# A fused encoder block in float32 on one core: which PSUM banks row tiles take, where x1's transposes stand, and the order of the last writes

## The chip, the cores and the metric

The kernel runs on one core of one Trainium2 chip. The metric is the device time of one execution in microseconds (us); the number that counts is the median over several executions. A profiled execution is one more execution, recorded instruction by instruction by the hardware profiler.

## The reference: what is computed

One layer of an encoder with two attention mixers side by side, for x of shape 1 x 512 x 2048 in float32:

```python
h = rmsnorm(x, g_mix)
qa, ka, va, qb, kb, vb = split(h @ w_in)          # 1024, 256, 256, 1024, 1024, 1024 columns
out_a = rmsnorm(mixer_a(qa, ka, va, g_q_a, g_k_a), g_out_a)   # 8 query heads, 2 kv heads, axial rotary
out_b = rmsnorm(mixer_b(qb, kb, vb), g_out_b)                 # 8 heads, three dilated windows, partial rotary
x = x + concat(out_a, out_b) @ w_out
h2 = rmsnorm(x, g_ffn)
gate, up = split(h2 @ w_gate_up)                  # D_FF = 5632
x = x + (silu(gate) * up) @ w_down
return rmsnorm(x, g_final)
```

The input's 512 rows are four row tiles of 128. A product in float32 precision is made of three passes: each operand is split into a high and a low part, and `mm3` (L229 to L231) issues high x high, high x low and low x high into one PSUM bank.

## The kernel before

**The work in its order.** The first chunk makes kA and vA from w_in. Three column blocks make qA, vB and half of qkB out of sums of blocks of the operands (seven products in place of eight). Two plain chunks of `in_chunk` make the rest of qkB: a chunk has 512 output columns, sixteen units (one slice of 128 rows of w_in each), and in each unit four row tiles, one `mm3` each into a bank of its own. Then come the products with w_out, four chunks c = 0 to 3 for mixer A's half (`out_chunk` "A", whose units hold one slice of eight) and four for B's. Gate and up, down, and the final norm follow, in column blocks again.

**Attention beside it.** The attention's tasks stand in a list called `side`. While plain chunks and out chunks run, `give` hands out credit (2.8 for a unit, half of it after the second row tile, the rest at the end), and takes tasks from the front of `side` as long as the credit covers their cost. A task of mixer A's heads is a slot (`head_slot`): a score product, the softmax of an earlier one, transposes of p (L659) into a bank called pt, which ScalarE (L220) and VectorE (L221) copy out as pTh and pTl, and the product of p with the values. `weighed` attaches a cost to a task; in `wait(n)` n empty tasks are put into the list, each worth a unit outside the attention, where one unit gives a credit of 1.

**Banks.** PSUM has eight banks of 128 x 512, all in one queue, `banks`. `bank()` takes the one at the left, which was given back longest ago; `release` appends at the right. It is a queue of the program as it is written out: a bank is given back at the place where the instruction that reads it last is issued, and a new product in it waits on the chip until that instruction has run. A chunk takes its four banks at its first unit; `in_chunk`'s post evicts by ScalarE (L491, evqkB), `out_chunk`'s by VectorE (L1195, which scales and adds to x1).

**x1 and its transposes.** Behind the last unit of an out chunk B, x1's 512 columns are done, and `h_side` (L1236) transposes them piece by piece on TensorE (L1241, four 128 x 128 transposes for a piece). ScalarE copies them into `pair` with a gain (L1244), VectorE sums blocks of two pieces (L380), and ScalarE and VectorE split these into high and low parts (L1252, L1254). These tasks go through `side` as well, behind `wait(2)` for c = 0 and 1 and `wait(1)` for c = 2 and 3.

**The start.** In the first sixteen units `prepare` makes the high parts of the weights on ScalarE (L963) and the low parts on VectorE (L966), and `row_squares` (L388) has ScalarE square the rows of x for the first norm.

**The end.** `finish` does the last product's row tile 1 by itself: ScalarE squares it (L1532), VectorE adds up (L1534), GpSimd takes the power -0.5 (L1535), which gives the row scale r, and then the four column groups of the last row tile are scaled and written: three by `write` (L1506 on VectorE or L1508 on ScalarE, DMA at L1509), one straight out of PSUM (L1538 and L1540, DMA at L1541).

Of the kernel before, what the change touches and what calls it, by code (L numbers as in the profile page):

```python
# [20 lines left out]
P = 128  # L21
# [56 lines left out]
def encoder_block(ctx, tc, x, w_in, g_q_a, g_k_a, w_out, w_gate_up, w_down, g_final, x_t, gains, c_ident, c_mask,  # L78
# [27 lines left out]

    def bank():
        return banks.popleft()

    def release(*tiles):  # L110
        banks.extend(tiles)
# [627 lines left out]
    def attention_tasks():  # L739
        def q_tasks(j):  # L740
            return norm_rope(lambda t: (qA[j][t], qA[j][t]), 4, "q")

        def both(cost, *lists):
            return [weighed(cost, lambda fs=fs: [f() for f in fs]) for fs in zip(*lists)]

        qA.update({j: {} for j in range(2)})
        qkB.update({j: {} for j in range(4)})
        push_heads()
        k_squares, k_turned, k_scaled = norm_rope(lambda t: (kA[t][:, :256], kA[t][:, 256:]), NKV, "k")
        q_squares, q_turned, q_scaled = q_tasks(0)  # L750
        vs = [lambda t=t: split_vA(t) for t in range(NT)]
        tables = light(0.8, table_tasks())
        todo = tables[:3] + both(1.4, [lambda t=t: scale_k(t) for t in range(NT)], k_squares)
        todo += both(0.6, vs) + tables[3:]
        todo += both(2.0, q_squares, k_turned, k_scaled) + both(2.6, q_turned, q_scaled)
        todo += light(0.6, [lambda kv=kv: transpose_k_a(kv) for kv in range(NKV)]) + [heads[0].tq, heads[0].tk]
        todo += light(0.1, [lambda: reload("qA1", qA[1])])
        extra = {}

        def at(slot, tasks):  # L760
            extra.setdefault(slot, []).extend(tasks)
        at(20, light(0.1, [lambda: nc.sync.dma_start(mask, c_mask)]))
        q_squares, q_turned, q_scaled = q_tasks(1)
        for t in range(NT):
            at(t // 2, both(0.8, q_squares[t:t + 1]))
            at(2 + 2 * t, both(0.9, q_turned[t:t + 1]))
            at(3 + 2 * t, both(0.9, q_scaled[t:t + 1]))
        def turn_at(turned, slots):
            for t, s in enumerate(slots):
                at(s, light(0.05, [lambda t=t: turned.part(t)]))  # L770
                at(s + 1, light(0.05, [lambda t=t: turned.turn(t)]))
        turn_at(turned_a[0], (0, 1, 2, 2))
        turn_at(turned_a[1], range(4, 12, 2))
        for j in range(4):
            s = NT * (NHA + 2 * j)
            if 2 * j < TURNED_ON_PE["B"]:
                at(s - 11, light(0.1, [lambda j=j: reload(f"qkB{j}", qkB[j])]))
                at(s - 7, light(0.9, [lambda j=j: rope_partial(qkB[j]["whole"])]))
                continue
            at(s - 16, light(0.1, [lambda j=j: reload(f"qkB{j}", qkB[j])]))  # L780
            for n in range(2):
                at(s - 13 + n, light(0.45, [lambda j=j, n=n: rope_partial(qkB[j]["whole"], 2 * n, 2)]))
            turn_at(turned_b[j], range(s - 10, s - 6))
        for h in range(NHB):
            s = NT * (NHA + h)
            at(s + 2, light(0.1, [lambda h=h: load_vB(h)]))
            at(s + 4, light(0.4, [lambda h=h: split_vB(h)]))
        for s in range(2 * NHA * NT + VALUE_LAG + 2):
            cost = 1.5 if s < NHA * NT else 1.2 if s < 2 * NHA * NT else 0.7
            todo += [weighed(cost, lambda s=s: head_slot(s))] + extra.get(s, [])  # L790
        return todo

# [52 lines left out]
    def in_chunk(pieces, post):  # L845
        box = {}

        def mm(u, k):
            if k == 0:
                box["ps"] = [bank() for _ in range(NT)]  # L850
            by_rows(u, k, KD, lambda i, w, t: mm3(box["ps"][t], x_of(i, t), w, i == 0, i == KD - 1),
                    lambda rows: post(box["ps"], rows))
        add_chunk(w_in, [k * P for k in range(KD)], pieces, mm, None, tag="wi")
# [295 lines left out]
    def out_chunk(kind, c):  # L1149
# [28 lines left out]
        def mm(u, n):  # L1178
            k = order[n]
            if n == 0:  # L1180
                box["ps"] = [bank() for _ in range(NT)]
                if kind == "A":
                    whole = slot("x1", F32, (P, NT, 512))
                    x1[c] = [whole[:, t] for t in range(NT)]
                    for t in range(NT):
                        nc.sync.dma_start(x1[c][t], x[0, t * P:(t + 1) * P, c * 512:(c + 1) * 512])
            by_rows(u, n, NHA, lambda i, w, t: mm3(box["ps"][t], cols(oS[kind, order[i]], t * P), w, i == 0,
                                                   i == NHA - 1), post, kind == "A")

        def post(rows):  # L1190
# [7 lines left out]
                if kind == "B" and c < NC - 1:  # L1198
                    square_x1(c, t)
            if kind == "B" and NT - 1 in rows:  # L1200
                wait(2 if c < 2 else 1)
                if c == NC - 1:
                    side.extend(lambda p=p: h_side(2 * c, p, True) for p in range(4))
                    side.append(lambda: [square_x1(c, t) for t in (0, 1)])
# [30 lines left out]
    def h_side(i, half, apart=False):  # L1235
        if half < 2:  # L1236
            k = 2 * i + half
            c, j = divmod(k, 4)
            ps = bank()
            for n, t in enumerate((2, 3, 0, 1) if half == 0 else range(NT)):  # L1240
                nc.tensor.transpose(ps[:, n * P:(n + 1) * P], x1[c][t][:, j * P:(j + 1) * P], ident)  # L1241
            if half == 0 and not hpart:
                hpart[0] = sp.tile([P, 4 * 512], F32, tag="pair", bufs=1, name=nm("pair"))
            nc.scalar.activation(hpart[0][:, half * 1024:half * 1024 + 512], ps, AF.Copy, scale=gf[:, k:k + 1])  # L1244
            release(ps)
# [272 lines left out]
    def finish(box):  # L1518
# [14 lines left out]
        r = fin["r", 1] = m[:, 1:2]  # L1533
        nc.vector.tensor_tensor(m[:, 3:], m[:, :1], pre[:, 1:], op=OP.add)  # L1534
        nc.gpsimd.tensor_tensor(r, m[:, 3:], mhalf[:, :1], op=OP.pow)  # L1535
        write(1, 0, True, nc.sync)
        write(1, 2, False, nc.scalar)
        nc.vector.tensor_tensor(m[:, 2:3], r, r2["r"][:, 1:2], op=OP.mult)  # L1538
        write(1, 1, True, nc.sync)
        nc.vector.scalar_tensor_tensor(x1[3, 1], ps[1], m[:, 2:3], gfin[3], op0=OP.mult, op1=OP.mult)  # L1540
        nc.scalar.dma_start(out[0, P:2 * P, 3 * 512:], x1[3, 1])  # L1541

    box.after("m3", 40, lambda: evs.extend(held[name][:, t] for name in ("s1", "s7") for t in range(2)))
    first = 0
# [77 lines left out]
    for n, u in enumerate(units):  # L1622
        share["now"], share["due"] = n, 1.0
        if n < KD:
            if n + 5 < KD:
                load_x(n + 5)
            if n + 1 < KD:
                x_prep(n + 1)
        if n <= ROWS_AT[-1]:
            row_squares(n)  # L1630
        prepare(n)
        for v in units[n + 1:n + 3]:
            if v.early is not None:
                v.early()
                v.early = None
        u.mm(u)
        if u.post is not None:
            u.post()
        for f in hooks.pop(n, ()):
            f()  # L1640
        give(1.0)
# [57 lines left out]
```

## Time and profile before

| what | value |
| --- | --- |
| median of 3 runs | 1947.94 us (1947.91 to 1948.31) |
| profiled execution, its own time | 1947.76 us |
| span of its records | 1946.0 us |
| TensorE (PE) busy | 1932.1 us, 99% |
| VectorE (DVE) busy | 1537.4 us, 79% |
| ScalarE (ACT) busy | 1152.7 us, 59% |

Rows of a timeline are: start, duration, engine, line of the kernel, operation, output <- input, form, and in brackets the idle time before it and what ended it. A row with xN holds N instructions that follow each other, and its duration spans them all. Matmuls overlap: a matmul's row is longer than its distance to the next, so idle time of TensorE is best read from start to start. A list of waits has engine, line, what was waited for, total us, times, longest us. A row of windows has the window, its length, then busy time and count of TensorE, its weight loads, VectorE, ScalarE and GpSimd, the granted clock of TensorE, the DMA share and the bytes per second.

### The profile page before, as it was taken

Reading aid. Unit: us, or ns where it says so; the run is one execution under the profiler, and the core shown is the slowest. Engines: PE = TensorE matmul, PEld = TensorE weight load, DVE = VectorE, ACT = ScalarE, POOL = GpSimd, SP = SyncE. Lnnn points to the kernel's source line nnn. Section 1 sums busy time; section 2 is a strip of 40 time slices with the busy share of each in tenths; the row PEclk is TensorE's granted clock in tenths of the full one; section 3 lists DMA queues with packets and bytes.
Section 4 is the critical chain, followed back from the end, with each engine's and each line's share of the span. In section 5 each row is a group of like instructions: output and inputs, shape, how many; then the busy total and the mean of one; then the engine's idle time right before and its main releaser. Section 6 shows DMA issues by size and latency. Waiting matters only on the chain.

```text
span 1946.0 us, 24535 instructions
## 1 busy us (share of the span) xinstructions
PE 1932.1 (99%) x8687; PEld 1593.4 (82%) x8687; DVE 1537.4 (79%) x2020; ACT 1152.7 (59%) x1673; POOL 140.6 (7%) x184
## 2 busy tenths in 40 slices
PE   9999999999999999999999999999999999999998
PEld 7888887888888888888888888888888888888886
DVE  7987768888785697778778778787788978787886
ACT  7755556675765565555555555555555666555555
POOL 1000011000000000000000000000000121111121
PEclk9999999999999999999999999999999999999999
DMA  9676694354442556858658768678587798868865
GB/s 347 235 263 225 216 290 118 92 184 146 124 147 98 174 196 204 284 144 286 241 164 284 225 195 285 196 231 296 145 283 269 215 243 266 230 162 243 239 146 168
DMA packets 268924, 413.50 MB, mean 212 GB/s; under 512 B 75584, under 2 KB 102720, under 8 KB 268672
## 3 DMA queue, kind: packets, MB, share of 16 engines
q1 hardware_dynamic: 237968, 325.31, 51.6%
q0 software_dynamic: 22480, 60.57, 12.4%
q10 hardware_dynamic: 8352, 26.05, 4.1%
q8 instruction: 68, 1.11, 0.2%
q14 instruction: 56, 0.46, 0.1%
HBM read 334.52 MB, written 62.65 MB: 204 GB/s over the span
## 4 chain that ended last, share of the span: by engine, by line
PE 94%; DVE 3%; ACT 2%; issue 1%; DMA 0%; ACTq 0%; DVEq 0%; POOLq 0%; POOL 0%; SPq 0%
PE b L229 31%; PE b L231 30%; PE b L230 30%; PE b L659 1%; ACT rj L448 0%; DVE x L1195 0%; PE b L1241 0%; DVE w L307 0%; DVE ra L461 0%; ACT w L302 0%; DVE tw L966 0%; DVE qA L464 0%; DVE qA L470 0%; DMA stage<-in_w_in_dram 0%; DVE fixed L635 0%
## 5 line engine op out<-in xcount | busy, mean ns | idle before, releaser
L907 ACT ACTIVATE wide<-raw 128x1024 fp32r<-128x1024 f32 x462 | 487.1, 1058 | 457.6 <-PE b L231 269.6
L910 DVE TENSOR_TENSOR wide<-raw,wide 128x1024 fp32r<-128x1024 f32 x462 | 562.8, 1223 | 202.8 <-ACT wide L907 191.5
L229 PE MATMUL b<-wide,arena 128*128 128x512 f32 x1848 | 719.8, 390 | 0.0
L231 PE MATMUL b<-wide,arena 128*128 128x512 f32 x1848 | 719.2, 389 | 0.0
L230 PE MATMUL b<-wide,arena 128*128 128x512 f32 x1848 | 719.1, 389 | 0.0
L231 PEld LDWEIGHTS b<-wide,arena 128*128 128x128 f32 x1848 | 346.9, 188 | 72.3
L230 PEld LDWEIGHTS b<-wide,arena 128*128 128x128 f32 x1848 | 346.9, 188 | 71.7
L229 PEld LDWEIGHTS b<-wide,arena 128*128 128x128 f32 x1848 | 346.9, 188 | 71.7
L1043 DVE TENSOR_TENSOR raw<-raw,raw 128x1024 f32<-128x1024 f32 x264 | 321.6, 1220 | 7.0 <-DMA raw<-in_w_gate_up_dram 7.0
L230 PE MATMUL b<-tw,arena 128*128 128x512 f32 x396 | 154.3, 390 | 0.6 <-DVE tw L966 0.6
L231 PE MATMUL b<-tw,arena 128*128 128x512 f32 x396 | 154.2, 389 | 0.0
L229 PE MATMUL b<-tw,arena 128*128 128x512 f32 x396 | 154.1, 389 | 0.0
L963 ACT ACTIVATE tw<-stage 128x512 fp32r<-128x512 f32 x140 | 85.5, 629 | 69.3 <-DVE stage L1043 45.9
L966 DVE TENSOR_TENSOR tw<-stage,tw 128x512 fp32r<-128x512 f32 x140 | 93.9, 688 | 22.1 <-ACT tw L963 15.9
L229 PE MATMUL b<-w,arena 128*128 128x512 f32 x240 | 95.2, 397 | 0.0
L231 PE MATMUL b<-w,arena 128*128 128x512 f32 x240 | 93.9, 391 | 0.0
L230 PE MATMUL b<-w,arena 128*128 128x512 f32 x240 | 93.5, 390 | 0.0
L230 PEld LDWEIGHTS b<-tw,arena 128*128 128x128 f32 x396 | 74.3, 188 | 16.7 <-DVE tw L966 1.4
L231 PEld LDWEIGHTS b<-tw,arena 128*128 128x128 f32 x396 | 74.3, 188 | 15.9 <-DVE arena L354 0.4
L229 PEld LDWEIGHTS b<-tw,arena 128*128 128x128 f32 x396 | 74.3, 188 | 15.5
L380 DVE TENSOR_TENSOR pair<-pair 128x256 f32<-128x256 f32 x120 | 46.4, 423 | 46.7 <-ACT pair L1244 23.2
L220 ACT ACTIVATE pTh<-b 128x512 fp32r<-128x512 f32 x64 | 38.3, 598 | 64.4 <-PE b L659 62.5
(243 smaller groups left out, 2118.1 us busy)
## 6 DMA issues: line engine op xcount, KB each, us to landing
raw<-in_w_gate_up_dram SPq DMA_DIRECT2D x308, 512.0 KB, 6.3
raw<-in_w_down_dram SPq DMA_DIRECT2D x88, 512.0 KB, 7.4
stage<-in_w_in_dram SPq DMA_DIRECT2D x111, 256.0 KB, 5.4
forms<-pair POOLq DMA_DIRECT2D x22, 896.0 KB, 6.3
fr<-forms ACTq DMA_DIRECT2D x35, 512.0 KB, 5.3
raw<-in_w_out_dram SPq DMA_DIRECT2D x32, 512.0 KB, 4.2
x1d<-s POOLq DMA_DIRECT2D x54, 256.0 KB, 6.5
stage<-in_w_in_dram SPq DMA_DIRECT2D x90, 128.0 KB, 3.6
```

Of the source, the lines that this page charges most:

```text
L220: nc.scalar.activation(hi, src, AF.Copy)
L229: nc.tensor.matmul(dst, ah, bh, start=start, stop=False, skip_group_check=chained)
L230: nc.tensor.matmul(dst, ah, bl, start=False, stop=False, skip_group_check=chained)
L231: nc.tensor.matmul(dst, al, bh, start=False, stop=stop, skip_group_check=chained)
L380: nc.vector.tensor_tensor(out, x, y, op=op)
L659: nc.tensor.transpose(ps[:, t * P:(t + 1) * P], self.p[t][:, kb * P:(kb + 1) * P], ident)
L907: nc.scalar.activation(self.hi, self.src, AF.Copy)
L910: nc.vector.tensor_tensor(self.lo, self.src, f32(self.hi), op=OP.subtract)
L963: nc.scalar.activation(self.pair[:, 0], self.src, AF.Copy)
L966: nc.vector.tensor_tensor(self.pair[:, 1], self.src, f32(self.pair[:, 0]), op=OP.subtract)
L1043: nc.vector.tensor_tensor(t[dst], t[src[0]], t[src[1]], op=OP.add if form == "m6" else OP.subtract)
```

## The change

The change has these parts:

- `chunk_banks` takes two banks from the left of the queue for row tiles 0 and 1, and the two that were given back last, from its right, for row tiles 2 and 3. `in_chunk` uses it, and `out_chunk` for mixer A from c = 1 on.
- In the attention's list the head slots 2, 3 and 4 cost 1.65 where they cost 1.5.
- The first head's `tq` (first query's transposes) and `tk` change places: a `tk` of 0.7, `tq`, and an empty task of 0.3, where there were two tasks of 1.0.
- `wait(2)` for c = 2, which had `wait(1)`.
- In `h_side` the four transposes of a piece run in the order of the row tiles; only where the results stand in the bank is turned.
- In the first units `row_squares` stands behind `prepare` from unit KD = 16 on, up to which it stands ahead of it.
- In `finish` the last row tile's writes have another order and other queues.

```diff
+    def chunk_banks():
+        first = [bank() for _ in range(2)]
+        late = [banks.pop() for _ in range(2)]
+        return first + late[::-1]
...
-        todo += light(0.6, [lambda kv=kv: transpose_k_a(kv) for kv in range(NKV)]) + [heads[0].tq, heads[0].tk]
+        todo += light(0.6, [lambda kv=kv: transpose_k_a(kv) for kv in range(NKV)])
+        todo += [weighed(0.7, lambda: heads[0].tk()), heads[0].tq, weighed(0.3, lambda: None)]
...
-            cost = 1.5 if s < NHA * NT else 1.2 if s < 2 * NHA * NT else 0.7
+            cost = 1.65 if 2 <= s < 5 else 1.5 if s < NHA * NT else 1.2 if s < 2 * NHA * NT else 0.7
...
-                box["ps"] = [bank() for _ in range(NT)]
+                box["ps"] = chunk_banks()
...
-                box["ps"] = [bank() for _ in range(NT)]
+                box["ps"] = chunk_banks() if kind == "A" and c > 0 else [bank() for _ in range(NT)]
...
-                wait(2 if c < 2 else 1)
+                wait(2 if c < NC - 1 else 1)
...
-            for n, t in enumerate((2, 3, 0, 1) if half == 0 else range(NT)):
+            for t in range(NT):
+                n = (t + 2) % NT if half == 0 else t
                 nc.tensor.transpose(ps[:, n * P:(n + 1) * P], x1[c][t][:, j * P:(j + 1) * P], ident)
...
+        nc.vector.tensor_tensor(m[:, 2:3], r, r2["r"][:, 1:2], op=OP.mult)
+        nc.vector.scalar_tensor_tensor(x1[3, 1], ps[1], m[:, 2:3], gfin[3], op0=OP.mult, op1=OP.mult)
+        write(1, 2, False, nc.sync)
+        nc.sync.dma_start(out[0, P:2 * P, 3 * 512:], x1[3, 1])
+        write(1, 1, False, nc.scalar)
         write(1, 0, True, nc.sync)
-        write(1, 2, False, nc.scalar)
-        nc.vector.tensor_tensor(m[:, 2:3], r, r2["r"][:, 1:2], op=OP.mult)
-        write(1, 1, True, nc.sync)
-        nc.vector.scalar_tensor_tensor(x1[3, 1], ps[1], m[:, 2:3], gfin[3], op0=OP.mult, op1=OP.mult)
-        nc.scalar.dma_start(out[0, P:2 * P, 3 * 512:], x1[3, 1])
...
-        if n <= ROWS_AT[-1]:
+        if n < KD:
             row_squares(n)
         prepare(n)
+        if KD <= n <= ROWS_AT[-1]:
+            row_squares(n)
```

**How the instructions move.** In the rows below b0 to b7 are the banks, and lines of the changed kernel are 5 to 9 higher for the same code (L229 becomes L234, L491 L496, L1195 L1201).

TensorE at the first unit of the second plain chunk, the first matmul of each product, before: first the last score product ahead of the chunk (with qTh), then row tiles 0 to 3 (with w), then the next score product.

```order
L229 MATMUL b4_75<-arena5_85,qTh_74_2663 128x512
...
L229 MATMUL b5_76<-w_84_2708,arena2_84 128x512
...
L229 MATMUL b6_77<-w_84_2708,arena2_84 128x512
...
L229 MATMUL b7_78<-w_84_2708,arena2_84 128x512
...
L229 MATMUL b0_71<-w_84_2708,arena2_84 128x512
...
L229 MATMUL b3_74<-arena5_85,qTh_80_2695 128x512
```

The same place after:

```order
L234 MATMUL b6_77<-arena5_85,qTh_74_2663 128x512
...
L234 MATMUL b1_72<-w_84_2708,arena2_84 128x512
...
L234 MATMUL b2_73<-w_84_2708,arena2_84 128x512
...
L234 MATMUL b4_75<-w_84_2708,arena2_84 128x512
...
L234 MATMUL b6_77<-w_84_2708,arena2_84 128x512
...
L234 MATMUL b7_78<-arena5_85,qTh_80_2695 128x512
```

Row tiles 0 to 3 had b5, b6, b7 and b0; now they have b1, b2, b4 and b6, and b6 is also the bank of the score product just ahead.

ScalarE up to that place, before: L448 squares qA's rows, L551 turns planes of it, L491 evicts the plain chunk before, L646 is the exponential of a score and L302 a weight's high part.

```order
L448 ACTIVATE rj_92_2753,fixed_81<-qA1_76_2667 128x128 x4
L551 ACTIVATE plane_94_2762<-qA0_34_2377 128x1024
L491 ACTIVATE evqkB2_95_2770<-b7_78,fixed_81 128x512
L491 ACTIVATE evqkB2_96_2773<-b0_71,fixed_81 128x512
L646 ACTIVATE p_97_2779,fixed_81<-b3_74,fixed_81 128x512
L302 ACTIVATE w_99_2788<-raw_64_2581 128x512
L551 ACTIVATE plane_102_2802<-qA0_34_2377 128x1024
L551 ACTIVATE plane_103_2804<-qA0_34_2377 128x1024
L491 ACTIVATE evqkB2_104_2812<-b1_72,fixed_81 128x512
L491 ACTIVATE evqkB2_105_2815<-b2_73,fixed_81 128x512
L646 ACTIVATE p_106_2821,fixed_81<-b4_75,fixed_81 128x512
```

After:

```order
L453 ACTIVATE rj_92_2753,fixed_81<-qA1_76_2667 128x128 x4
L556 ACTIVATE plane_94_2762<-qA0_34_2377 128x1024
L496 ACTIVATE evqkB2_95_2770<-b7_78,fixed_81 128x512
L496 ACTIVATE evqkB2_96_2773<-b0_71,fixed_81 128x512
L651 ACTIVATE p_97_2779,fixed_81<-b5_76,fixed_81 128x512
L307 ACTIVATE w_99_2788<-raw_64_2581 128x512
L556 ACTIVATE plane_102_2802<-qA0_34_2377 128x1024
L556 ACTIVATE plane_103_2804<-qA0_34_2377 128x1024
L496 ACTIVATE evqkB2_104_2812<-b3_74,fixed_81 128x512
L496 ACTIVATE evqkB2_105_2815<-b4_75,fixed_81 128x512
L651 ACTIVATE p_106_2821,fixed_81<-b6_77,fixed_81 128x512
```

Nothing changes its place. The four evictions read b7, b0, b1 and b2 before, and b7, b0, b3 and b4 now, and the exponential behind them reads b4 before and b6 now.

TensorE at the first unit of out chunk A, c = 1, again the first matmul of each product, before: transposes of p (L659) into pt, the product of p with the values, the transposes of a query (L590), and the four row tiles.

```order
L659 MATMUL b5_76<-fixed_81,p_295_3928 128x128
L229 MATMUL b6_77<-pTh_315_4102,vh_302_3997 128x512
...
L590 MATMUL b2_73<-fixed_81,qkB1_267_3733 128x128 x4
L229 MATMUL b3_74<-arena2_84,arena5_85 128x512
...
L229 MATMUL b4_75<-arena2_84,arena5_85 128x512
...
L229 MATMUL b7_78<-arena2_84,arena5_85 128x512
...
L229 MATMUL b0_71<-arena2_84,arena5_85 128x512
```

After:

```order
L664 MATMUL b2_73<-fixed_81,p_295_3928 128x128
L234 MATMUL b6_77<-pTh_315_4102,vh_302_3997 128x512
...
L595 MATMUL b7_78<-fixed_81,qkB1_267_3739 128x128 x4
L234 MATMUL b1_72<-arena2_84,arena5_85 128x512
...
L234 MATMUL b5_76<-arena2_84,arena5_85 128x512
...
L234 MATMUL b2_73<-arena2_84,arena5_85 128x512
...
L234 MATMUL b7_78<-arena2_84,arena5_85 128x512
```

Row tiles 2 and 3 had b7 and b0; now they have b2 and b7, the banks of the transposes of p and of the query just ahead.

VectorE around x1's last columns, before: L380 sums blocks of two pieces of c = 2, L1254 makes their low parts, L910 makes low parts of gate and up weights, and the four L1195 evict out chunk B, c = 3.

```order
L380 TENSOR_TENSOR pair_501_5413<-pair_501_5413 128x256 x4
L307 TENSOR_TENSOR w_557_5846<-raw_533_5671,w_556_5845 128x512
L1254 TENSOR_TENSOR arena2_84<-pair_501_5413,arena2_84 128x2x256
L1254 TENSOR_TENSOR arena5_85<-pair_501_5413,arena5_85 128x5x256
L910 TENSOR_TENSOR wide_560_5873<-raw_546_5771,wide_559_5872 128x1024
L910 TENSOR_TENSOR wide_562_5875<-raw_549_5798,wide_561_5874 128x1024
L1195 SCALAR_TENSOR_TENSOR x1_403_4784<-b6_77,fixed_81,x1_403_4784 128x512
L1195 SCALAR_TENSOR_TENSOR x1_403_4784<-b7_78,fixed_81,x1_403_4784 128x512
```

After (L385, L312, L1261, L916 and L1201 are the same lines):

```order
L312 TENSOR_TENSOR w_557_5841<-raw_533_5671,w_556_5840 128x512
L385 TENSOR_TENSOR pair_501_5413<-pair_501_5413 128x256 x4
L916 TENSOR_TENSOR wide_560_5864<-raw_546_5766,wide_559_5863 128x1024
L1261 TENSOR_TENSOR arena2_84<-pair_501_5413,arena2_84 128x2x256
L1261 TENSOR_TENSOR arena5_85<-pair_501_5413,arena5_85 128x5x256
L916 TENSOR_TENSOR wide_562_5866<-raw_549_5789,wide_561_5865 128x1024
L1201 SCALAR_TENSOR_TENSOR x1_403_4784<-b7_78,fixed_81,x1_403_4784 128x512
L1201 SCALAR_TENSOR_TENSOR x1_403_4784<-b0_71,fixed_81,x1_403_4784 128x512
```

L307 has moved ahead of the sums, and one L910 stands between them and the low parts, where it stood behind these.

## The prediction

> **What bounds the kernel now.** I read the page first, then TensorE's list of waits, then the timelines around each place at which the changed order of instructions meets a wait. The page's first lines:
>
> ```profile
> span 1946.0 us, 24535 instructions
> PE 1932.1 (99%) x8687; PEld 1593.4 (82%) x8687; DVE 1537.4 (79%) x2020; ACT 1152.7 (59%) x1673; POOL 140.6 (7%) x184
> ```
>
> TensorE is busy for 1932.1 of 1946.0 us and the change leaves every matmul in place, so it can only move the few microseconds in which TensorE stands still. The profiled execution took 1947.76 us: 1.76 lie around its span, and the median of the runs shown (1947.94) is 0.18 above it. 0.2% of that is 3.9 us, about what a measurement of this kernel can tell from no change. TensorE's waits, as engine, line, what it waited for, total, times, longest:
>
> ```profile
> PE b L187 <- DVE warm L182: 1.3, 1, 1.3
> PE b L659 <- DVE x L1195: 1.2, 2, 0.6
> PE b L860 <- DVE tw L1615: 0.7, 1, 0.7
> PE b L659 <- DVE p L654: 0.7, 1, 0.7
> PE b L590 <- DVE qA L471: 0.6, 1, 0.6
> PE b L230 <- DVE tw L966: 0.6, 2, 0.3
> PE b L1241 <- DVE x L1195: 0.5, 2, 0.3
> ```
>
> Five of the seven are what the edits reach (L187 and L860 belong to the start). Together they show 3.6 us; counted from start to start of the matmuls, as below, about 5. That is about all there is to win, while a bank that comes free late has no such ceiling. So each edit is judged by who read the bank last that a row tile now gets.
>
> **The change part by part.** *Banks of the second plain chunk (chunk_banks in in_chunk; head slots 2 to 4 at 1.65).* The rows are the stretch around its first matmuls, as busy times of the engines, then ScalarE's evictions, then TensorE:
>
> ```profile
> 318.00:334.00 16.00, 15.59 (x71) 12.59 (x69) 10.38 (x23) 16.00 (x54) 5.08 (x5) 1.00 0.49 119
> ```
>
> ```profile
> 331.53 1.27 ACT L491 ACTIVATE evqkB<-b,fixed 128x512 f32<-128x512 f32 x2
> 332.67 0.70 ACT L646 ACTIVATE p<-b,fixed 128x512 f32<-128x512 f32 x1
> ```
>
> ```profile
> 329.00 0.39 PE L229 MATMUL b<-w,arena 128*128 128x512 f32 x1
> 329.69 0.39 PE L229 MATMUL b<-w,arena 128*128 128x512 f32 x1
> 333.10 0.49 PE L659 MATMUL b<-fixed,p 128*128 128x128 f32 x3
> 334.31 0.33 PE L659 MATMUL b<-fixed,p 128*128 128x128 f32 x1 [0.72 <-DVE p L654]
> ```
>
> 329.00 and 329.69 are the first matmuls of row tiles 2 and 3 (three matmuls apart: 0.23 each). Before, they take b7 and b0, evicted as the chunk's first two. In the changed order they take b4 and b6: b4 is read by the fourth eviction, the second of the pair at 331.53, which ends at 332.80; b6 by the exponential that ends at 333.37. ScalarE is busy for all 16.00 of these 16 us (fourth number of the first row) and nothing in its order ahead of that eviction changes, so the eviction can't come earlier. TensorE, at 329.00, waits until about 332.85: 3.85 us, and some 0.1 more for the restart. Row tile 3 comes 0.69 later, after the exponential. What goes is the wait at 334.31: the fourth of these transposes begins 1.21 after the first, where three steps of 0.11 (an estimate, half of a 512-column matmul) would be 0.33, so 0.88 is won, because p is long done when a late TensorE reaches it behind the product that the new costs put first. Net 3.85 + 0.1 - 0.88 = **+3.1**. Bounds: -0.9, if the banks come free in time after all, and +4.0, if p still waits. I take the sum, since the order and the rows leave no other work to run there.
>
> *The same in out chunks A, c = 1 to 3.* At c = 1, VectorE and TensorE:
>
> ```profile
> 467.40 0.68 DVE L221 TENSOR_TENSOR pTl<-b,pTh 128x512 fp32r<-128x512 f32 x1
> 468.31 0.69 DVE L224 SCALAR_TENSOR_TENSOR arena<-b,arena 128x512 fp32r<-128x512 f32 x1 [0.23 <-ACT arena L223]
> ```
>
> ```profile
> 467.00 0.39 PE L229 MATMUL b<-arena,arena 128*128 128x512 f32 x1
> 467.69 0.39 PE L229 MATMUL b<-arena,arena 128*128 128x512 f32 x1
> ```
>
> The tiles of rows 2 and 3 (467.00, 467.69) change from banks that L1195 had left to b2, which pTl reads until 468.08, and b7, which the turned query reads until 469.00. The first waits 1.13, the second, now due at 468.82, another 0.23, and the restart is 0.1: **+1.5** (0 to +1.6). At c = 2 and 3:
>
> ```profile
> 500.07 0.39 PE L231 MATMUL b<-arena,arena 128*128 128x512 f32 x1
> 501.95 0.66 PE L659 MATMUL b<-fixed,p 128*128 128x128 f32 x4 [0.59 <-DVE x L1195]
> ```
>
> ```profile
> 537.60 0.39 PE L231 MATMUL b<-arena,arena 128*128 128x512 f32 x1
> 539.58 0.66 PE L659 MATMUL b<-fixed,p 128*128 128x128 f32 x4 [0.60 <-DVE x L1195]
> ```
>
> Four steps of 0.23 lie between these rows, 0.92, and they take 1.88 and 1.98. The score tile and the transposes of p now have banks that were left earlier, and the row tiles behind them take the two that L1195 leaves. They are due some 0.15 us after that: **-1.0 and -1.1** (-0.5 at worst for each, as they may wait a part of it).
>
> *wait(2) for c = 2, and x1's transposes in the order of rows.* TensorE where the transposes wait, and VectorE ahead of the second place:
>
> ```profile
> 655.23 0.28 PE L1241 MATMUL b<-fixed,x 128*128 128x128 f32 x1
> 655.70 0.55 PE L1241 MATMUL b<-fixed,x 128*128 128x128 f32 x3 [0.19 <-DVE x L1195]
> 678.73 0.55 PE L1241 MATMUL b<-fixed,x 128*128 128x128 f32 x3 [0.33 <-DVE x L1195]
> 679.03 0.47 PE L229 MATMUL b<-wide,arena 128*128 128x512 f32 x1
> ```
>
> ```profile
> 669.32 1.55 DVE L380 TENSOR_TENSOR pair<-pair 128x256 f32<-128x256 f32 x4 [3.41 <-ACT pair L1244]
> 670.79 0.69 DVE L307 TENSOR_TENSOR w<-raw,w 128x512 fp32r<-128x512 f32 x1
> 672.28 1.49 DVE L1254 TENSOR_TENSOR arena<-pair,arena 128x1280 fp32r<-128x1280 f32 x1 [0.20 <-ACT arena L1252]
> 675.96 2.72 DVE L1195 SCALAR_TENSOR_TENSOR x<-b,fixed,x 128x512 f32<-128x512 f32 x4
> ```
>
> The wait at 655.70 goes (0.47 from start to start, less 0.11: -0.36). But all of c = 2's transposes come one unit later, 12 matmuls or 2.7 us, so L380 starts near 672.0 - 0.36. From 669.32 to the evictions at 675.96 VectorE takes 6.64; less the 0.6 of L307, which now stands ahead, and the idle 0.20, 5.8 is left. The four L1195 then run from about 677.5 to 680.2, where they ended at 678.68, and c = 3's transposes (already late before) need them all. Taking rows in order lets three of four transposes go while the last eviction runs, so the next product follows at about 680.4 in place of 679.03: **+1.3** with the 0.36 counted in. Bounds: -1.0, if both waits go, and +2.0. I take the sum, as the order of VectorE is fixed.
>
> *Without effect.* The first query's transposes: two tasks of cost 1.0 become 0.7, 1.0 and 0.3, the sum and every engine's order stay, so the wait on qA L471 stays: 0. The row squares behind prepare change ScalarE's order alone; the waits for L966 there are VectorE's:
>
> ```profile
> 53.00:63.50 10.50, 10.20 (x45) 7.94 (x43) 10.43 (x23) 8.18 (x17) 0.00 (x0) 1.00 0.83 281
> ```
>
> VectorE (third busy time) has 10.43 of 10.50 us of work in an unchanged order: 0, at best -0.6 by the list. In the attention between 400 and 460 us, products and transposes of p change places; the list has no wait from there above 0.5: 0, within 0.5 either way.
>
> *The end.* The last writes, with their issue:
>
> ```profile
> 1939.59 0.72 ACT L1508 ACTIVATE x<-x,fixed 128x512 f32<-128x512 f32 x1 [0.85 <-POOL fixed L1535]
> 1939.59 0.49 DVE L1506 TENSOR_SCALAR x<-x,fixed 128x512 f32<-128x512 f32 x1 [0.66 <-POOL fixed L1535]
> 1939.99 0.15 DVE L1538 TENSOR_TENSOR fixed<-fixed 128x1 f32<-128x1 f32 x1
> 1940.10 0.81 SPq L1509 DMA_DIRECT2D out_dram<-x  x2
> 1940.46 0.75 DVE L1540 SCALAR_TENSOR_TENSOR x<-b,fixed,gfin 128x512 f32<-128x512 f32 x1
> 1941.23 0.34 ACTq L1541 DMA_DIRECT2D out_dram<-x  x1
> ```
>
> Now L1538 goes first (1939.59) and L1540 ends near 1940.53, but SP's queue has ScalarE's column ahead of it (1940.31), and two scalings follow: ScalarE's second until 1941.03 and VectorE's L1506 until 1941.02. The last issue moves from 1941.23 to about 1941.1, the first from 1940.10 to 1940.34. By the last, -0.1; by the first, +0.24: I take **+0.1**, -0.5 to +0.5. The Trainium skill (DMA: Bandwidth & Descriptors, Issuing engines are not separate DMA queues) says that spreading issues over engines saves issue time only; by that the order of queues is worth no more than one issue, 0.34 to 0.4 in these rows, and the sum stands.
>
> Sum: 3.1 + 1.5 - 1.0 - 1.1 + 1.3 + 0.1 = +3.9, of which I give 0.2 back as waits later in the attention shrink behind a TensorE that is 3 us late: **+3.7**. On the profiled execution that is 1951.5, as a median **1951.6 us**. It is just below what can be told from no change (1951.8).
>
> **The rivals.** *The new waits don't bite (faster).* If ScalarE's evictions and VectorE's come free in time, only the gains stand: -0.88, -2.1, -1.0 and the end at -0.3, 4.3 in all: 1943.7. For it speaks that all four waits that are aimed at are real; against it that ScalarE has not a tenth of a microsecond to spare between 318 and 334.
>
> *The clock falls in the long wait (slower).* 3.85 us would be the longest idle time of TensorE behind the start. How it runs from rest shows in the warm-up:
>
> ```profile
> L187 PE MATMUL b<-warm x7: 608/634/635, 1.3 to 3.8; 128*128 128x512 bf16 x7
> ```
>
> Six steps from 1.3 to 3.8 are 0.42 each, against 0.23: if the wait puts TensorE back there for as many matmuls, it loses 6 x 0.19 = 1.1 us, and 1.4 if for the length of seven. With +3.7 that is +5.0: 1952.9. It decides if the wait is long enough to count as rest; the granted clock is 1.00 in both stretches quoted, and no row has a wait between 1.3 and 3.85. The Trainium skill (TensorE: Matmul & The Clock Gate, HAM oscillation) puts the point at about 3.4 us, in a window that runs free of the program, which a wait of 3.85 only sometimes fills; by it the time would be this rival's in some runs, by the rows quoted (1.00 throughout) the sum's.
>
> *It does less than it says (no change).* Two edits move nothing, and the long wait may be given back: a TensorE 3 us late finds qkB's and c = 1's evictions done, so the +1.5 and the +1.3 don't come, and the gains of 2.1 stand: 3.1 - 2.1 = +1.0, 1948.9. Against it: both engines' work there is released by TensorE itself and comes late with it.
>
> **How the numbers follow.** My sum 0.57, no bite 0.15, the clock 0.13, given back 0.15. The sum's own spread (the bounds of x1's +1.3 and of c = 1 above all, some 1.5 us either way) puts 0.32 of its 0.57 below 1951.8 and 0.25 above. Faster: 0.12, most of the first rival. Same: 0.32 + 0.15 + 0.03 = 0.50. Slower: 0.25 + 0.13 = 0.38. The range runs from 1944.0, which leaves out over half of the first rival, to 1953.8, beyond which lie some of the clock's cases and a sum in which p's wait stays too.
>
> **What would show it.** In the profile after, TensorE should wait close to 3.9 us for ScalarE's L491 (L496 by its new number) near 329, and no longer for p there; for VectorE's pTl some 1.1 near 470; not at all for L1195 at 503 and 541; and about 2 us at x1's transposes near 681. The qA wait of 0.6 and the two for tw should still be there. I am wrong if the first of these is missing, or if the granted clock behind it is below 1.00.

## The result, and the profile after

The changed kernel takes 1956.2 us (median of 6, 1955.43 to 1957.16), the kernel before, run again beside it, 1948.12 (median of 6, 1947.69 to 1950.89): ratio 1.0038, 95% interval 1.0025 to 1.0051. It is slower than every case of the prediction, and outside its range (1944.0 to 1953.8). The profiled execution took 1955.92 us with a span of 1954.1, 8.1 above that of before. The page and TensorE's list of waits after:

```profile
span 1954.1 us, 24530 instructions
PE 1935.6 (99%) x8687; PEld 1596.3 (82%) x8687; DVE 1537.1 (79%) x2019; ACT 1153.1 (59%) x1674; POOL 140.4 (7%) x184
```

```profile
PE b L234 <- ACT evqkB L496: 3.7, 1, 3.7
PE b L1248 <- DVE x L1201: 1.5, 4, 0.5
PE b L192 <- DVE warm L187: 1.3, 1, 1.3
PE b L866 <- DVE tw L1622: 1.0, 1, 1.0
PE b L234 <- DVE pTl L226: 0.9, 1, 0.9
PE b L235 <- DVE tw L972: 0.6, 2, 0.3
PE b L595 <- DVE qA L476: 0.6, 1, 0.6
```

The new waits are the forecast ones: for the fourth eviction, for pTl and for x1; those for qA and tw are still there, as forecast. TensorE is also busy for 3.5 us longer with the same 8687 matmuls: the list can't show that part, but start to start does. TensorE's timeline at the second plain chunk's wait and behind it, and a window of the stretch behind it (its last three columns are granted clock, DMA share, GB/s):

```profile
331.23 0.39 PE L236 MATMUL b<-w,arena 128*128 128x512 f32 x1
335.30 0.79 PE L234 MATMUL b<-w,arena 128*128 128x512 f32 x1 [3.68 <-ACT evqkB L496]
335.89 0.63 PE L235 MATMUL b<-w,arena 128*128 128x512 f32 x1
337.59 0.63 PE L236 MATMUL b<-w,arena 128*128 128x512 f32 x1
338.02 0.50 PE L234 MATMUL b<-arena,qTh 128*128 128x512 f32 x1
```

```profile
335.50:338.00 2.50, 2.50 (x6) 1.94 (x7) 0.00 (x1) 0.93 (x3) 0.66 (x2) 0.50 1.12 212
```

From 331.23 to 335.30 are 4.07 us where one step of 0.23 is due: 3.84 lost. The six steps from 335.30 to 338.02 take 2.72 in place of 1.36, at a granted clock of 0.50: 1.4 more. The Trainium skill (TensorE: Matmul & The Clock Gate, HAM oscillation) has this rule, that the clock falls to half after some 3.4 us of idle time; here the trace agrees, with 3.68 us of it, but a run below falls with less. Then TensorE's timeline at the first unit of all, the first product's twelve matmuls, before and after, with the window of these matmuls after:

```profile
5.15 2.98 PE L860 MATMUL b<-tw,arena 128*128 128x512 f32 x12 [0.72 <-DVE tw L1615]
```

```profile
5.43 5.37 PE L866 MATMUL b<-tw,arena 128*128 128x512 f32 x12 [1.00 <-DVE tw L1622]
```

```profile
5.00:10.60 5.60, 5.17 (x12) 4.12 (x13) 3.71 (x6) 3.19 (x5) 0.71 (x1) 1.00 0.99 357
```

The same twelve matmuls take 5.37 us, 2.4 more, and start 0.28 later. The clock column shows 1.00 there only because the trace's first record of the clock is its rise to full, at 10.55 us, and the column reads 1.00 where there is no record; the pace has to be read from the starts. TensorE's timelines at out chunk A, c = 1 and then c = 2; then at x1's transposes of c = 3, first the last matmul ahead of them before, then after:

```profile
473.83 0.40 PE L236 MATMUL b<-arena,arena 128*128 128x512 f32 x1
475.17 0.51 PE L234 MATMUL b<-arena,arena 128*128 128x512 f32 x1 [0.95 <-DVE pTl L226]
476.03 0.50 PE L234 MATMUL b<-arena,arena 128*128 128x512 f32 x1
509.24 0.39 PE L236 MATMUL b<-arena 128*128 128x512 f32 x1
509.47 0.60 PE L664 MATMUL b<-fixed,p 128*128 128x128 f32 x4
```

```profile
677.74 0.39 PE L231 MATMUL b<-wide,arena 128*128 128x512 f32 x1
```

```profile
683.77 0.39 PE L236 MATMUL b<-wide,arena 128*128 128x512 f32 x1
684.64 0.33 PE L1248 MATMUL b<-fixed,x 128*128 128x128 f32 x1 [0.48 <-DVE x L1201]
686.61 0.33 PE L1248 MATMUL b<-fixed,x 128*128 128x128 f32 x1 [0.33 <-DVE x L1201]
686.70 0.48 PE L234 MATMUL b<-wide,arena 128*128 128x512 f32 x1
```

From 473.83 to 476.03 four steps take 2.20 in place of 0.92, with the restart behind it 1.4 in all. At c = 2 the transposes of p follow without a wait (509.24, 509.47). At x1 the stretch from the last matmul to the product behind the transposes is 2.93 (683.77 to 686.70); before it was 1.29 (677.74 to 679.03), so 1.64 is lost, less the 0.4 won at 655.

By the start of one and the same matmul in both traces, the 8.1 us come from: the first unit +2.4, the second plain chunk +5.35 for its wait and -0.96 for p, c = 1 +1.4, c = 2 and 3 -1.0 each, x1 +1.2, the end +0.2, and 0.5 in small pieces (0.2 in the attention up to 455 us, 0.2 near 1490).

### The profile page after: what moved, and what is told of

It reads as the page before. It is cut to its first block, busy times and chain, and to the rows that moved or that the text cites. A ratio compares the mean times of both kernels' runs of the same rounds, so it can differ in the third digit from the quotient of the medians.

```text
span 1954.1 us, 24530 instructions
## 1 busy us (share of the span) xinstructions
PE 1935.6 (99%) x8687; PEld 1596.3 (82%) x8687; DVE 1537.1 (79%) x2019; ACT 1153.1 (59%) x1674; POOL 140.4 (7%) x184
## 4 chain that ended last, share of the span: by engine, by line
PE 88%; issue 8%; DVE 2%; POOL 1%; DMA 1%; ACT 0%; SPq 0%; POOLq 0%; DVEq 0%; ACTq 0%
PE b L234 29%; PE b L236 29%; PE b L235 29%; PE b L664 1%; PE b L1248 0%; DMA raw<-in_w_in_dram 0%; POOL fixed L216 0%; DVE x L1201 0%; PE b L866 0%; POOL qkB L487 0%; DVE tw L972 0%; DMA stage<-in_w_in_dram 0%; DVE w L312 0%; POOL oA L684 0%; DVE arena L1261 0%
## 5 line engine op out<-in xcount | busy, mean ns | idle before, releaser
L916 DVE TENSOR_TENSOR wide<-raw,wide 128x1024 fp32r<-128x1024 f32 x462 | 561.8, 1221 | 200.9 <-ACT wide L913 196.2
L234 PE MATMUL b<-wide,arena 128*128 128x512 f32 x1848 | 719.7, 389 | 0.0
L234 PEld LDWEIGHTS b<-wide,arena 128*128 128x128 f32 x1848 | 346.9, 188 | 71.7
L234 PE MATMUL b<-tw,arena 128*128 128x512 f32 x396 | 154.1, 389 | 0.0
L234 PE MATMUL b<-w,arena 128*128 128x512 f32 x240 | 96.0, 400 | 3.7 <-ACT evqkB L496 3.7
L234 PEld LDWEIGHTS b<-tw,arena 128*128 128x128 f32 x396 | 74.5, 188 | 15.7
L385 DVE TENSOR_TENSOR pair<-pair 128x256 f32<-128x256 f32 x120 | 46.4, 421 | 48.2 <-ACT pair L1251 24.7
```

The source lines that it names most:

```text
L234: nc.tensor.matmul(dst, ah, bh, start=start, stop=False, skip_group_check=chained)
L385: nc.vector.tensor_tensor(out, x, y, op=op)
L916: nc.vector.tensor_tensor(self.lo, self.src, f32(self.hi), op=OP.subtract)
```

## The experiments

Two things had to be told apart: what the banks cost and what the clock adds, and whether the slow first unit belongs to the change at all. Theory A: a rest of TensorE lowers its clock, at the start in some executions of any kernel, behind the long wait always. (For the long wait this held; at the start the clock turned out not to fall but to rise late.) The rivals are in the expectations. The kernel before ran beside each set: medians 1949.1 (27 executions), 1949.3 (26) and 1949.5 (19). Its single times fall into two groups, 1947.6 to 1948.5 and 1949.1 to 1950.5, and the upper one is the larger in each set. The 1947.94 ahead of the prediction is the median of three times of the lower group; of the six beside the result, two are of the upper one (1949.84 and 1950.89).

**The two edits of the plain chunk alone** (e1_ramp_only):

```diff
-                box["ps"] = [bank() for _ in range(NT)]
+                box["ps"] = chunk_banks()
...
-            cost = 1.5 if s < NHA * NT else 1.2 if s < 2 * NHA * NT else 0.7
+            cost = 1.65 if 2 <= s < 5 else 1.5 if s < NHA * NT else 1.2 if s < 2 * NHA * NT else 0.7
```

> The kernel before with chunk_banks in in_chunk and the new costs of head slots 2 to 4, nothing else. Theory A (banks that come free late, then a clock that falls in the wait): a wait of 3.8 us for the fourth eviction at the second plain chunk, a granted clock near 0.5 for the 2 to 3 us behind it that costs 1.5 us, and 0.9 us won on p, so 4.4 us over before: about 1952.5 us, and matmuls of the first unit at the pace of before. Rival B (the lower clock there comes from somewhere else in the change): 3.0 us over before, 1951.1. Rival C (the slow first matmuls of the changed kernel come with its banks): 2.4 us more, 1954.9.

Measured: 1953.99 us (1952.52 to 1955.62), ratio 1.0025 (1.0015 to 1.0035). The wait is there in TensorE's list, and two windows behind it show the clock:

```profile
PE b L234 <- ACT evqkB L496: 3.7, 1, 3.7
```

```profile
333.00:335.50 2.50, 2.50 (x7) 1.92 (x8) 0.00 (x0) 0.90 (x3) 0.64 (x2) 0.50 1.10 214
335.50:338.00 2.50, 2.50 (x7) 1.97 (x6) 0.95 (x3) 0.26 (x1) 0.00 (x0) 0.50 1.04 301
```

The half clock lasts for twelve matmuls and more here, over 5 us, where the changed kernel's trace had 2.7: the chunk costs 6.6 in this trace against 5.35, though the wait is the same. The clock comes with the wait (rival B falls). This execution had the quick first unit, so these banks don't always bring the slow one (rival C); e7 below has it without them.

**The changed kernel without these two edits** (e2_after_old_ramp), the same diff taken back:

> The changed kernel with in_chunk's banks and the head slots' costs as before. Theory A: the wait, the slow matmuls behind it and the gain on p all go, 4.4 us under the changed kernel: about 1951.8 us if its first matmuls stay slow, about 1949.4 if these come and go from execution to execution and this one is free of them. The other waits stay: 1.1 us for pTl at out chunk A, c = 1, and four of 0.5 at x1's transposes. Rival B (the clock is not from the wait): 3.0 under, 1953.2.

Measured: 1951.32 us (1948.62 to 1952.41), 4.9 under the changed kernel, ratio to before 1.0011 (1.0002 to 1.0021). The profiled execution, with a quick first unit, is 2.6 over before's span though its waits are those forecast. The reason is at x1's transposes, where the clock fell as well; TensorE's timeline:

```profile
677.69 0.33 PE L1248 MATMUL b<-fixed,x 128*128 128x128 f32 x1 [0.48 <-DVE x L1201]
679.75 0.75 PE L234 MATMUL b<-wide,arena 128*128 128x512 f32 x1
680.30 0.63 PE L235 MATMUL b<-wide,arena 128*128 128x512 f32 x1
680.72 0.63 PE L236 MATMUL b<-wide,arena 128*128 128x512 f32 x1
682.43 0.98 PE L1248 MATMUL b<-fixed,x 128*128 128x128 f32 x4
```

Four scattered waits of under 0.5 us with single transposes between them were enough: 0.43 from 680.30 to 680.72. x1 costs 3.25 here where it cost 1.64 in the changed kernel's trace, which has the same four waits; what tells the two apart is shown with the shorter wait below.

**The wait filled** (e3_after_filled):

```diff
+                if i == 0 and t == 2 and name == "qkB3":
+                    for _ in range(5):
+                        mm3(box["ps"][0], x_of(0, 0), w, False, False)
                 mm3(box["ps"][t], x_of(i, t), w, i == 0, i == KD - 1)
```

> The changed kernel, but the product of row tile 0 is issued five more times ahead of row tile 2 at the first unit of the second plain chunk, into row tile 0's bank: 15 matmuls or 3.4 us in the 3.8 us for which TensorE waits (the sum in that bank, and so a part of qkB, is wrong). Theory A (idle time lowers the clock): the wait shrinks to about 0.4 us, the eviction that ends it stays in its place, the granted clock stays at 1.00 and the 1.5 us behind the wait are not lost: 1.5 under the changed kernel, about 1954.7 us. Rival (the slow matmuls there are slow for another reason, their operands or the transfers of that stretch): same time as the changed kernel, 1956.2, with matmuls at 0.43 behind the wait.

Measured: 1954.14 us (1952.14 to 1955.28), 2.1 under the changed kernel, with 15 matmuls more. TensorE's timeline at the end of the wait, and the window behind it:

```profile
333.75 0.39 PE L236 MATMUL b<-w,arena 128*128 128x512 f32 x1
334.42 0.50 PE L234 MATMUL b<-w,arena 128*128 128x512 f32 x1 [0.29 <-ACT evqkB L496]
334.76 0.40 PE L235 MATMUL b<-w,arena 128*128 128x512 f32 x1
```

```profile
334.40:337.00 2.60, 2.58 (x11) 2.09 (x12) 0.42 (x2) 1.16 (x3) 0.90 (x2) 1.00 1.11 225
```

0.23 from start to start and a clock of 1.00. Nothing else differs at that place, so it is the rest that lowers the clock; the operands and transfers are the same. The median mixes executions with either pace of the first unit (the profiled one had 0.43), but the chunk by itself can be compared: wait, clock and p together cost 3.06 in this trace against 4.41 in the changed kernel's, 1.35 less where 1.5 was forecast.

**A shorter wait** (e6_after_wait32): in the second plain chunk the bank given back last is put back to the queue's end.

```diff
+        newest = banks.pop()
+        late = [banks.pop() for _ in range(2)]
+        banks.append(newest)
```

> The changed kernel, but in the second plain chunk the bank given back last stays in the queue and row tiles 2 and 3 take the two given back before it, the third and the fourth eviction's: TensorE waits 3.2 us in place of 3.85 for the same ScalarE. Theory A (the clock falls once a whole stretch of about 3.4 us is idle, so that 3.2 is too short): granted clock 1.00 behind the wait, 0.65 less wait and 1.4 to 2.8 less behind it, about 1953.5 us. Rival (any wait of this order lowers it, as the scattered waits at x1's transposes do in some executions): 0.43 from start to start behind this wait too, only 0.65 won, 1955.3 us.

Measured: 1956.13 us (1954.63 to 1956.76, 5 executions), no gain over the changed kernel. TensorE's timeline behind a wait whose idle time the trace gives as 3.11, and two windows, the first up to the place where the clock falls, the second as long as it is low:

```profile
332.73 0.79 PE L241 MATMUL b<-w,arena 128*128 128x512 f32 x1 [3.11 <-ACT evqkB L503]
333.33 0.63 PE L242 MATMUL b<-w,arena 128*128 128x512 f32 x1
```

```profile
328.66:332.07 3.41, 0.96 (x5) 0.46 (x3) 3.34 (x9) 3.41 (x7) 2.55 (x3) 1.00 0.61 154
332.07:338.89 6.82, 6.16 (x15) 4.80 (x16) 3.22 (x8) 3.55 (x9) 1.09 (x2) 0.50 1.04 262
```

The clock falls all the same, for 13 matmuls, and it falls within the wait, at 332.07, 0.66 us before the wait ends.

The limit of 3.4 us that I took from the Trainium skill is not the limit here: theory A stands, its number falls. The Trainium skill (TensorE: Matmul & The Clock Gate, Part 1, What's actually happening) also says that the clock is decided over windows that run free of the program, and the traces show this grid. In all twelve, the times between two changes of the clock are whole multiples of 3.413 us (but for the low clock behind the last matmul, which the end cuts off): in the changed kernel it rises at 10.55, falls at 334.82 (95 stretches of 3.413 later) and is back at 338.23 (one more). Two stretches of this grid in the changed kernel, ahead of its fall and at x1's transposes, where it did not fall; then e2_after_old_ramp's at x1, ahead of its fall and behind it; then the one of e10_query_later in which TensorE stood still most without a fall:

```profile
331.41:334.82 3.41, 0.20 (x1) 0.00 (x0) 3.23 (x8) 3.41 (x7) 1.79 (x3) 1.00 0.77 213
682.98:686.39 3.41, 2.16 (x9) 1.05 (x7) 3.41 (x5) 0.00 (x0) 0.00 (x0) 1.00 0.00 0
```

```profile
676.37:679.79 3.42, 1.95 (x9) 0.92 (x7) 3.42 (x6) 0.00 (x0) 0.00 (x0) 1.00 0.00 0
679.79:683.20 3.41, 3.41 (x12) 2.72 (x12) 0.95 (x1) 0.69 (x1) 0.00 (x0) 0.50 0.00 0
```

```profile
446.50:449.91 3.41, 2.05 (x14) 1.44 (x12) 3.31 (x10) 1.45 (x5) 0.00 (x0) 1.00 0.26 77
```

The second number is TensorE's busy time. Between the first rise and the last matmul the clock falls seven times in the twelve traces, each time at the end of a stretch in which TensorE was busy for 0.20 to 1.95 us; in every other stretch at full clock it was busy for 2.05 or more. So in these traces it is the busy share of one stretch that decides, and not an unbroken rest, with a limit between 1.95 and 2.05 by this view.

A wait of 3.7 us leaves one of the stretches it touches busy for at most 1.6 (an estimate from its length alone) and brings the fall wherever it lies; the four waits at x1 bring it only where nearly all of them lie in one stretch (1.95 in e2 and 1.94 in e3, against 2.16, 2.42 and 2.42 in the changed kernel, e4 and e6). The half clock then holds for one stretch (the changed kernel, e2, e3, e7) or two (e1, e4, e6). Where the grid lies differs between executions, and so does the price of one and the same wait.

**Nine warm-up matmuls**, in the changed kernel (e4_after_warm9) and in the one before (e5_before_warm9):

```diff
-    warm_up(7)
+    warm_up(9)
```

> The changed kernel with nine warm-up matmuls in place of seven. Theory A (the first matmuls run slow since TensorE rested for 1.6 us between the warm-up and the first weights): the rest shrinks to about 0.8 us, the twelve matmuls of the first unit run at 0.23 in place of 0.43, 2.4 us under the changed kernel: about 1953.8 us. Rival (these matmuls wait for their operands, or the pace is set before): no difference, 1956.2 us, with 0.43 from start to start as before.

> The kernel before with nine warm-up matmuls in place of seven. Its own times fall into two groups, 1947.6 to 1948.2 and 1949.1 to 1950.5. Theory A (the upper group is executions in which the first weights come a little later and the first twelve matmuls run at 0.43 in place of 0.23, whatever the kernel does later): the longer warm-up leaves less rest ahead of them, the times lie in the lower group alone, median about 1947.6 us. Rival (the upper group comes from elsewhere, the transfers of the whole stream for one): two groups again, median near 1949.

Measured: the changed kernel 1955.21 us (1954.43 to 1955.9), 1.0 less; the one before 1947.97 (1947.69 to 1948.43), all ten in the lower group, ratio 0.9993 (0.9984 to 1.0002). TensorE's timeline at the changed kernel's start shows the first product at nearly the full pace:

```profile
1.26 3.57 PE L192 MATMUL b<-warm 128*128 128x512 bf16 x9 [1.26 <-DVE warm L187]
5.01 3.00 PE L866 MATMUL b<-tw,arena 128*128 128x512 f32 x12 [0.18 <-DVE tw L1622]
```

So the upper group is the slow first unit, it belongs to both kernels, and the 2.4 us of it in the profile above is no effect of the change. (No trace of the kernel before from its upper group was kept; e7, which leaves the start as it was, has a first product at 0.43, which costs 1.8 us.) It is not the length of the rest that decides, as theory A had it: with seven warm-up matmuls TensorE's idle time ahead of the first product is 0.67 to 0.77 us in the four traces whose first product ran at 0.23 and 0.56, 0.64 and 1.00 in the three where it ran at 0.43. The warm-up itself runs at 0.43, and the first record of the clock in each trace is its rise: at 3.95 to 4.88 us in those four, at 9.23 to 10.55 in those three, and at 4.24 to 6.77 in the five traces with nine, of which four still have two to four first steps at or near 0.43. That the changed kernel won only 1.0 goes with what the traces show behind the long wait: in the three with a quick first unit (e1, e4, e6) the half clock lasted for two stretches, in the one without it for one, 12 or 13 matmuls against 5.

**wait(2) alone** (e7_wait_only):

```diff
-                wait(2 if c < 2 else 1)
+                wait(2 if c < NC - 1 else 1)
```

> The kernel before with wait(2) for c = 2 and nothing else. Theory A (the sums for c = 2 now stand on VectorE ahead of c = 3's evictions): the wait of 0.36 us at 655 goes, the transposes near 680 wait until the last eviction at about 680.2, in one long wait for the third one and one for the last, and the region costs +1.2 to +1.4 us, and some 1.6 more in executions in which the clock falls in it: 1949.2 to 1950.9 with the fast first matmuls. Rival (the loss there comes from the order of rows): no loss from the wait alone, the 0.36 is won, 1947.6.

Measured: 1951.24 us (1950.56 to 1952.92), ratio 1.0014 (1.0004 to 1.0023). TensorE's timeline has one long wait and one short, as forecast, and the window behind them the lower clock:

```profile
681.35 0.33 PE L1241 MATMUL b<-fixed,x 128*128 128x128 f32 x1 [1.79 <-DVE x L1195]
682.01 0.90 PE L1241 MATMUL b<-fixed,x 128*128 128x128 f32 x3 [0.33 <-DVE x L1195]
```

```profile
683.00:685.20 2.20, 2.20 (x6) 1.58 (x6) 0.09 (x1) 0.63 (x1) 0.00 (x0) 0.50 0.00 0
```

The region costs 3.05 in this trace, and the first unit at 0.43 costs 1.8 more. The loss is that of the wait edit, not of the order of rows.

**Only what paid** (e8_late_banks): `chunk_banks` for mixer A's out chunks with c > 1, x1's transposes in the order of rows, nine warm-up matmuls.

```diff
-                box["ps"] = [bank() for _ in range(NT)]
+                box["ps"] = chunk_banks() if kind == "A" and c > 1 else [bank() for _ in range(NT)]
...
-    warm_up(7)
+    warm_up(9)
```

> The kernel before with three parts: chunk_banks in out chunk A for c = 2 and 3 only, the transposes in the order of rows, and nine warm-up matmuls. Theory A: the two waits for L1195 at 501 and 539 go (1.0 us each) and nothing new waits, the transposes of c = 3 wait 0.2 less, and the first matmuls run fast: 1945.6 us, 2.3 under before's lower group. Rival (the banks are missed elsewhere, at the chunks behind): the 2.0 come back as waits between 540 and 600, 1947.6 us.

Measured: 1945.49 us (1945.33 to 1946.1), ratio to before 0.9982 (0.9972 to 0.9991): faster than both kernels, and steady. Nine warm-up matmuls alone gave 1947.97, so the banks and the order of rows are worth 2.5; by trace 1.0 at c = 2, 1.0 at c = 3 and 0.4 at x1. Its list has no wait for L1195 (here L1200) ahead of transposes of p, and none in their place.

**With the head slots' costs on top** (e9_plus_cost: 1.65 for slots 2 to 4), **and the first query's transposes really moved** (e10_query_later):

```diff
-        todo += light(0.6, [lambda kv=kv: transpose_k_a(kv) for kv in range(NKV)]) + [heads[0].tq, heads[0].tk]
+        todo += light(0.6, [lambda kv=kv: transpose_k_a(kv) for kv in range(NKV)])
+        todo += [weighed(2.8, lambda: heads[0].tq()), weighed(0.0, lambda: heads[0].tk())]
```

> The kernel of late banks (banks from the right for c = 2 and 3 only, x1's transposes in the order of rows, nine warm-up matmuls) with head slots 2 to 4 at 1.65. Theory A (the wait for p at 333 goes since two products now stand ahead of its transposes, not since TensorE is late): 0.9 us won with no long wait ahead, 1944.6 us, TensorE's list without p L654's 0.7. Rival (p is ready in time only for a TensorE that has waited 3.8 us before, so the gain in the changed kernel was a part of its loss): the wait for p stays, or another takes its place behind the moved products, 1945.5 us.

> The same with a cost of 2.8 on the first query's transposes and 0 on the task behind them, which moves these transposes behind two products of the plain chunk and nothing else; the change's own edit there moves nothing. Theory A: the wait of 0.7 us for qA L471 near 313 goes, another 0.7 won, 1943.9 us. Rival (the score behind them, or ScalarE's copy of the turned query, is late in its place): as without it, 1944.6 us.

Measured: 1946.29 us (1945.76 to 1946.82) and 1953.39 us (1952.9 to 1953.65). Theory A's times fail in both. With the costs, the wait for p goes and one for pTl comes two products later, while VectorE works through qA's rotation (L466 to L469): the rival's mechanism, so the gain on p in the changed kernel was a part of its loss. The loss of 0.8 over e8_late_banks is more than the rival had; in the trace it is 1.1, 0.4 of it by 700 us and 0.6 near 1490, far behind the edit, which stays open. TensorE's timeline:

```profile
338.94 0.50 PE L234 MATMUL b<-pTh,arena 128*128 128x512 f32 x1 [1.07 <-DVE pTl L226]
```

With the query moved, the wait for qA goes too, but the edit moves more than was expected of it: the tasks behind shift, and TensorE's list fills with later waits, 7.1 us more than with the costs alone, which neither theory had:

```profile
PE b L234 <- DVE fixed L644: 3.0, 3, 1.4
PE b L234 <- DVE x L1200: 1.5, 1, 1.5
PE b L664 <- DVE p L659: 1.0, 1, 1.0
```

## Why the prediction was wrong

- **The sum's step for the second plain chunk failed by a term.** The wait was right (3.85 forecast, 3.84 measured), and so was p (-0.88, -0.96). What the sum left out is the clock behind the wait, 1.4 to 2.8 us by trace, which the prediction held as a rival at 0.13 with 1.1 to 1.4. It came in all four traces with a wait of 3.1 us or more that was not filled. The rival's price was too small as well: it took the length from the warm-up's count of matmuls, and the half clock holds for one or two stretches of 3.41 us; nor does a wait have to fill such a stretch, as the prediction took it. I took "no row has a wait between 1.3 and 3.85" for a reason to leave it out; it was a reason to have no opinion. The rows quoted with a clock of 1.00 were from stretches without a long rest.
- **The start was not in the prediction at all.** The kernel before has executions that are some 1 to 3 us longer, through its first unit (1.5 to 2.4 in the three traces whose first product ran at 0.43), and three times and one profile of its lower group hid this. It isn't the change's.
- **c = 1** (+1.5 forecast, +1.4), **c = 2 and 3** (-1.0 and -1.1, -1.0 each): right in mechanism and size. The gain on **p** was right in size, but it is there only behind the long wait (e9).
- **x1** (+1.3): right in mechanism; +1.2 in the trace of the changed kernel, but +2.8 to +3.0 in traces in which the clock falls there. The +2.0 that bounded it took no account of the clock.
- **The end** (+0.1 from -0.1 and +0.24): +0.25 (8.70 to 8.73 us from the last matmul's start to the end in the five traces with the new order, 8.43 to 8.47 in the seven with the old). That is the size of the first issue's delay; the last issue hardly moved.
- **Without effect**: the waits for qA and tw are unchanged, as forecast.
- **"Given back"**, the third rival at 0.15, and the 0.2 that the sum gave back: nothing was; the attention from 342 to 455 us cost 0.2 instead. The prediction's own argument against this rival, that these engines are released by TensorE itself, fits.

Together: 3.7, and 1.4 to 4.4 for the clock at two places, gives 5.1 to 8.1 over the kernel before. Against the medians of 1949.1 to 1949.5, the changed kernel's 1956.2 is 6.7 to 7.1 over.

## What to carry to other kernels

Ask of a bank not when it came back to the queue but who reads it last and how much that engine has ahead: the newest bank paid (1.0 us, twice) where row tiles came just behind the evictions that freed it, cost 1.4 us at c = 1, where the engines that read these banks were 1.1 us behind, and 3.8 us where the evicting engine was 4 us behind. Price waits of TensorE that add up to some 1.5 us within 3.4 with the half clock behind them, and fill them or split the work so that they don't arise. Before reading one profile as the kernel, look at whether its single times fall into groups.

## What the runs showed of the hardware

In these twelve traces TensorE's clock changes only at the ends of stretches of 3.41 us, on a grid that lies elsewhere in each execution. It fell to half behind each stretch in which TensorE was busy for at most 1.95 us (seven of them) and behind none in which it was busy for 2.05 or more, whether the rest was in one piece (3.1 us of idle time), in two (1.8 and 0.33 with a single transpose between) or in four waits of under 0.5 us within 2.6 us, which did it in two traces and not in three others. The wait of 1.0 us at c = 1 never did it. The half clock then holds for one or two stretches, 5 to 13 matmuls of 512 columns; in the three traces with two, TensorE was busy for 2.58 to 2.79 us of the first, in the others for 2.93 or more. At the start no such limit can be read: the clock rose behind a stretch with 2.69 us busy in one trace, and not behind one with 2.85 in another. There, seven warm-up matmuls left it open whether the first product ran at 0.23 or 0.43; two more settled it but for its first steps. The granted clock's column shows the falls later in the program (0.50) but not the slow start (1.00 at 0.43 a matmul).
